# One planner setting: every engine's instruction order from the second machine model

## The chip, the cores and the metric

The program runs on one core of one Trainium2 chip. A core has five instruction streams that matter here: PE (TensorE, the matrix products; PEld is its weight loads), DVE (VectorE), ACT (ScalarE), POOL (GpSimd) and SP (SyncE, which here does nothing but issue DMA transfers). Each stream works off its own list in the order written into the program and waits at semaphores for the others. The metric is the device time in microseconds (us), from runs of one program.

## The reference, cut to what matters

One inference step of a two-layer trunk on 640 tokens (128 prompt, 512 latent) with 1024 features. For each layer: a normalised and modulated input `h`; one combined input projection `h @ w_in`; four token mixers side by side (a Mamba-2 scan, a retention, a grouped-query attention, a latent attention); each one's output times `w_br`, scaled by a sigmoid gate `h @ w_merge`, summed and multiplied by `w_out`; then a gated feed-forward with a width-3 convolution. The modulation is `silu(cond) @ w_mod + b_mod` with a `w_mod` of 1024 x 6144 per layer and two condition vectors.

```
h = rmsnorm(x, g_pre_mix) * (1 + sc_a) + sh_a
m = sum over 4 branches of sigmoid(h @ w_merge_b) * (branch_b(h) @ w_br_b)
x = x + g_a * rmsnorm(m @ w_out)
h = rmsnorm(x, g_pre_ffn) * (1 + sc_f) + sh_f
u = dwconv3(h @ w_ffn_up);  x = x + g_f * rmsnorm((silu(gate) * up) @ w_ffn_down)
```

## The kernel before

Activations lie feature-major: tiles of 128 features by 640 tokens. Every float32 operand of a linear layer is split exactly into a high and a low part, and a product is three matmuls of 320 columns (`lin_fm`, `lin_half`): high weights with both parts of the input, low weights with the high part. The weights come in 128 x 512 tiles: `weights` loads one from DRAM (`wr`, SP's queue, four buffers), ACT copies its high part (`wh`, line 305, four buffers), POOL subtracts for the low part (`wl`, line 308, three buffers). All matmuls are issued on line 321 (`mm`). Their results go to four PSUM banks (`lin`); three more (`st`) and one (`pv`) serve everything else.

The order of the program text is: the layer's input norm, the scan, the retention, the merge of branch 0, attention, merge 1, latent attention, merge 2, then `merge_out` (merge of branch 3, the output projection, two norms) and `ffn`. Two things are laid in between by hand:

- Steps that wait on a long chain (sums of a norm, chunks of the scans) are put on a list, `self.later`, and issued after a counted number of products of a linear layer (`go_on`; the constants `WAIT`, `RST`, `RHD`, `AWT`, `SWAIT`). The attention heads (`heads`, `head`, `maxima`) alternate the scores of one head with the row maxima of the next.
- The modulation products of later blocks are computed on DVE as a filler, two multiply-and-sum parts for each half row block (`mod_units`, line 584, output `wj`). Layer 1's modulation belongs to layer 0's last stages: `merge_out` and `ffn` call `fill(n)` at many places, and each half block's weights arrive in a tile `g` (five buffers) by a load on SP's queue, the queue that brings the `wr` tiles too.

What stands in the text is not yet the order on the chip. The library's planner takes the traced instructions and their dependencies, plays them on a model of the machine, and lists each engine's instructions (SP's loads among them) in the order in which the model started them. It does this twice: once taking ready instructions in the order of the text, and then, with each instruction's latest harmless start worked out from the first play, taking the ready one with the earliest of these. An instruction that is ready may so overtake others traced before it. Only two things hold it: data dependencies (a buffer's reuse is one of them), and order edges written by hand with `tc.issue_after`. All buffer counts are given in the kernel, so the planner does not choose them.

The edges are few. The helpers that write them are `go_on` and `behind` for PE and `fill`, which holds the filler's DVE work back only until the last input norm is done:

```
    def behind(self, on=True):
        return self.tc.issue_after(self.pe) if on else nullcontext()
```

```
        with self.tc.issue_after(self.last) if self.last is not None else nullcontext():
            for _ in range(n):
                if next(self.filler, 0) == 0:
                    break
```

Of the kernel before, what the change touches and what calls it, by code (L numbers as in the profile page):

```python
# [12 lines left out]
PSUM = bass.MemoryType.PSUM  # L13

D = 1024
T = 640
TP = 128
TL = 512
L = 2
# [7 lines left out]
# ---------------------------------------------------------------- host layout  # L27
FM_COLS = (
    [(512 + 128 * i, 128) for i in range(4)]        # 0-3   xs
    + [(1024, 128), (1152, 128)]                    # 4,5   B, C  # L30
    + [(128 * i, 128) for i in range(4)]            # 6-9   z
    + [(1296 + 128 * i, 128) for i in range(2)]     # 10,11 rq
    + [(1552 + 128 * i, 128) for i in range(2)]     # 12,13 rk
    + [(1808 + 128 * i, 128) for i in range(4)]     # 14-17 rv
    + [(2320 + 128 * i, 128) for i in range(4)]     # 18-21 rg
    + [(2832 + 128 * i, 128) for i in range(4)]     # 22-25 aq
    + [(3344, 128), (3472, 128)]                    # 26,27 ak, av
    + [(3600 + 128 * i, 128) for i in range(3)]     # 28-30 mcq
    + [(3984 + 128 * i, 128) for i in range(2)]     # 31,32 ckv
# [65 lines left out]
def _blk(w):  # L105
    """[L, K, M] -> [L, M/128, 128, K/128 * 128] (partition = k within its tile)."""
    l, k, m = w.shape
    return np.ascontiguousarray(
        w.reshape(l, k // 128, 128, m // 128, 128).transpose(0, 3, 2, 1, 4).reshape(l, m // 128, 128, k)
    )  # L110


def _cols(v):
    """[L, n*128] -> [L, 128, n]"""
    return v.reshape(v.shape[0], -1, 128).transpose(0, 2, 1)
# [98 lines left out]
# ---------------------------------------------------------------- the kernel  # L214
# [21 lines left out]
class Net:  # L236
# [14 lines left out]
    # ---- small helpers  # L251
# [83 lines left out]
    # ---- weights: float32 from DRAM, split exactly into two float32r parts  # L335
# [9 lines left out]
    def lin_fm(self, src, kt, xh, xl, m=128, unit=4, halves=((0, 320), (320, 640))):  # L345
        """w^T x by token halves: (PSUM [m, 320], their columns); src [128, kt * m] in DRAM, xh/xl lists of [128, tokens]"""
        p = [self.bank()[:m, : b - a] for a, b in halves]
# [14 lines left out]
    def lin_half(self, src, kt, xh, xl, m, done, hvs=(0,)):  # L362
        """done(w^T x [m, 320], half) for some token halves"""
# [17 lines left out]
    def lin_misc(self, src, kt, xh, xl, m, done, hvs=(0,)):  # L381
        """like lin_half for 48 outputs, the weights' two parts side by side: their products with xh in one pass,
        rows 0:48 and 64:112"""
# [22 lines left out]
    def lins(self, specs, full=0):  # L406
        """several linears whose first token half is wanted early: specs (src, kt, xh, xl, m, done);
        the first half of all of them comes first, the last one's weights serve both halves"""
# [9 lines left out]
    # ---- per-token factors from per-token sums, spread over the partitions  # L418
    def rsq(self, dst, src, scale, eps, mult=1.0):
        """dst = mult * (scale * src + eps)^-1/2 on small tiles"""  # L420
        m2 = 1.0 / (mult * mult)
        self.tsc(dst, src, scale * m2, eps * m2, ALU.mult, ALU.add)
        n = 1
# [7 lines left out]
    def rowsum(self, ss, scale, eps, mm=None, mult=1.0):  # L431
        """[128, 5]: mult * (scale * sum over the partitions + eps)^-1/2 per token"""
# [8 lines left out]
    def rowsum_later(self, ss, scale, eps, then):  # L441
        """then(R): the factors of the sums, spread, in steps between the products of other linears"""
# [16 lines left out]
    def spread(self, R, r, n):  # L459
        """R[p, 128 c + i] = r[i, c] on each partition p"""  # L460
# [8 lines left out]
    def selb(self, h):  # L469
        """[48, 128]: picks row h for the first 64 columns, row 8 + h for the others (rows 32.. the low parts)"""  # L470
        t = self.sbt(128, "selb", 2, F32R)
        self.act(t[:48].rearrange("p (a b) -> p a b", a=2), self.C("sel48", 48)[:, h : h + 9 : 8].unsqueeze(2).to_broadcast([48, 2, 64]))
        return t[:48]

    # ---- start
# [10 lines left out]
    def first(self):  # L486
        """x and the first norm: hh + hl = rmsnorm(x) * Am + S. S and Am come from TensorE, two feature tiles at a time,
        with silu(cond) [128, 2] as stationary"""
# [63 lines left out]
    # ---- modulation: silu(cond) @ w_mod, one output feature per partition  # L552
# [3 lines left out]
    def mod_units(self, l, blocks, halves, tile, pool=()):  # L556
        """the products of some output blocks, a part at a time"""
# [30 lines left out]
    def fill(self, n):  # L588
        """the next n parts of the filler, on DVE behind what it must not delay"""
# [8 lines left out]
    def mod_get(self, j, raw):  # L598
        """[128, 8, 2] of the six parts: product + bias"""
# [21 lines left out]
    # ---- norms  # L621
    def ss_add(self, ss, src, first, v=None):
        """ss += src^2"""
# [7 lines left out]
    def rs_half(self, sss, hv, scale, eps, then, mult=1.0, wait=5):  # L631
        """then(PSUM [128, 320]: mult * (scale * sum over the partitions of the sss + eps)^-1/2 of the half's tokens),
        in steps between the products of other linears"""
# [18 lines left out]
    def go_on(self, mm):  # L652
        """once per k tile of the linears, behind its products mm: a step that has waited long enough"""
# [13 lines left out]
    def flush(self, hvs=(0, 1)):  # L667
        """the steps left of some token halves"""
# [8 lines left out]
    def pre_half(self, x, sss, A, S, hh, hl, hv):  # L677
        """rmsnorm(x) * A + S of a token half, split"""
# [13 lines left out]
    def sq_add(self, sss, x, k, c):  # L692
        """the squares of x[k], added to the part of the engine that takes k"""
# [7 lines left out]
    def post_half(self, x, mo, ss, G, hv, then, squares=True, mult=1.0, old=None):  # L701
        """x = old (or x) + G * rmsnorm(mo / mult) of a token half; then(the new sums of squares)"""
# [14 lines left out]
    # ---- softplus on small tiles: max(x,0) + log1p(exp(-|x|))  # L717
# [17 lines left out]
    def conv_put(self, buf, p, hv):  # L735
        """half of a linear's output for the conv: prompt at 1..128, latent at 130..641, zeros around them"""
# [8 lines left out]
    def conv(self, buf, taps, bq):  # L745
        """centred width-3 conv over the tokens; the result has 641 columns: prompt at 0..127, latent at 129..640"""
# [12 lines left out]
    def silu_half(self, out, y, n, eng=None):  # L759
        """y holds half of the argument: out = (tanh(y) + 1) * y"""  # L760
# [4 lines left out]
    # ---- branch A  # L765
    def ssd(self, l, hh, hl):
# [5 lines left out]
        # dt  # L772
# [50 lines left out]
        # B, C  # L823
# [29 lines left out]
        # x  # L853
# [15 lines left out]
        # states  # L869
# [31 lines left out]
        # heads  # L901
# [46 lines left out]
    def gates(self, src, blocks, d):  # L948
        """2 * silu of a linear's outputs, kept in DRAM"""
# [31 lines left out]
    # ---- rope on [n, 512] latent columns  # L981
    def rotate(self, out, src, n, half, new=None):
        """out = src * cos + partner(src) * sin; src, out [n, 512]"""
# [8 lines left out]
    # ---- branch B  # L992
    def ret_in(self, l, hh, hl):
# [10 lines left out]
        # token-major, centred over the head's 128 values; those of the prompt also as they are  # L1004
# [17 lines left out]
    def ret_states(self, l, qk, vt):  # L1022
# [3 lines left out]
        # decays  # L1026
# [27 lines left out]
        # states  # L1054
# [52 lines left out]
    def ret(self, l, q, k, vt, Sin, Dr, QD, zd):  # L1107
        self.ph("ret.hd%d" % l)
        # heads by chunks; the outputs token-major, normalised as they are transposed
# [60 lines left out]
    # ---- attention over one head: queries q0:q0+nq, key tiles kts; scores^T = sum of lhsT/rhs pairs  # L1170
    def negmax(self, pairs, q0, nqt, k0, k1):
        """[128, nqt] = -max over keys k0..k1 of the scores, queries q0 + 128 i on partitions"""
# [15 lines left out]
    def maxrow(self, dst, nm, nqt, r0):  # L1188
        """dst [1, 128 nqt] (partition r0) = the columns of nm"""
# [6 lines left out]
    def probs(self, p, n, scale):  # L1196
        """exp(scale * p), split"""
# [8 lines left out]
    def maxima(self, kk, qq, q2, r0, wait):  # L1206
        """row r0 of q2 = -max of a head's scores per query, by steps"""
# [10 lines left out]
    def head(self, pairs, vh, vl, OP, SM, r_, scale, lag):  # L1218
        """a head's values and sums over the key tiles by steps; the latent's queries (columns 128:640) see the key columns
        128:768, the prompt's 0:128"""  # L1220
# [33 lines left out]
    def heads(self, n, maxima, head):  # L1254
        """the heads, each beside the maxima of the next one"""
# [7 lines left out]
    def attn_out(self, OP, SM, od, b, l, name):  # L1263
        """divide by the sums"""
# [5 lines left out]
    # ---- branch C  # L1270
    def att_in(self, l, hh, hl):
# [25 lines left out]
        # values  # L1297
# [13 lines left out]
    def att(self, l, raw, avT, r, od):  # L1311
# [27 lines left out]
        # normalised q, k  # L1339
# [54 lines left out]
    # ---- branch D  # L1394
    def mla_in(self, l, hh, hl):
# [3 lines left out]
        # low-rank q  # L1399
# [21 lines left out]
        # low-rank kv  # L1421
# [33 lines left out]
        # keys and values of all heads  # L1455
# [21 lines left out]
    def mla(self, l, qd, kd, vd, od):  # L1477
# [3 lines left out]
        # shared rotary key  # L1481
# [325 lines left out]
```

## Time and profile before

| what | us |
|---|---|
| three runs | 3084.05, 3086.69 (median), 3091.55 |
| the profiled execution, first to last instruction (span) | 3082.1 |
| PE busy in it | 2908.6 |
| DVE busy | 2002.3 |
| ACT busy | 1384.7 |
| POOL busy | 1141.6 |

The profiled execution is known by its span alone; the median of the runs is 4.6 us above it, which is what lies ahead of the first and behind the last instruction together with the difference from run to run. Busy time of PE is the union of its matmuls, which overlap each other; where it equals the length of a stretch, PE was never without a matmul in it. A wait is put down to the instruction that ended it.

### The profile page before, as it was taken

The page shows a single profiled execution, that of the slowest core. Times are in us where ns is not written, and L with a number is a line of the kernel's source. Part 1 is how long each engine was busy: PE and PEld are TensorE (multiplying, and loading weights), DVE is VectorE, ACT ScalarE, POOL GpSimd, SP SyncE. Part 2 cuts the span into 40 slices and gives each one's busy share as a digit, 9 for nine tenths or more (in the row PEclk, how much of TensorE's full clock was granted, in tenths as well). Part 3 has the DMA queues.
Part 4 walks back from the last instruction along what each step waited for, and adds up shares of the span by engine and source line. Part 5 has one row for each costly group of instructions (what it writes and reads, how often), then busy time and mean ns, then how long its engine had stood idle before and what let it go on. Part 6 is the DMA issues. An engine that isn't in the chain of part 4 may idle for free. (4 is left out here: it accounts for less than half of the span.)

```text
span 3082.1 us, 50945 instructions
## 1 busy us (share of the span) xinstructions
PE 2908.6 (94%) x18638; PEld 2721.2 (88%) x18638; DVE 2002.3 (65%) x3758; ACT 1384.7 (45%) x3013; POOL 1141.6 (37%) x889
## 2 busy tenths in 40 slices
PE   8999999999988988899988999999999999999998
PEld 4888898898888988899988899988988988999997
DVE  3678727637996599975576872177377455755556
ACT  3435246657634532233355353366476445433333
POOL 1223341131146643333364233411321566433334
PEclk9999999999999999999999999999999999999999
DMA  6215421143364435432243133211332433222223
GB/s 207 72 49 178 152 85 40 55 134 117 118 211 159 137 104 173 150 104 75 73 132 103 58 113 106 86 40 47 112 130 82 143 120 115 93 75 74 76 76 108
DMA packets 193418, 329.71 MB, mean 107 GB/s; under 512 B 20880, under 2 KB 54288, under 8 KB 193168
## 3 DMA queue, kind: packets, MB, share of 16 engines
q1 hardware_dynamic: 193168, 326.46, 32.5%
q8 instruction: 146, 2.39, 0.3%
q14 instruction: 104, 0.85, 0.1%
HBM read 293.41 MB, written 32.96 MB: 106 GB/s over the span
## 5 line engine op out<-in xcount | busy, mean ns | idle before, releaser
L308 POOL TENSOR_TENSOR wl<-wr,wh 128x512 fp32r<-128x512 f32 (+2 forms) x790 | 1068.9, 1357 | 1821.4 <-PE lin L321 1223.3
L321 PE MATMUL lin<-ah,wh 128*128 128x320 f32 (+1 forms) x3776 | 1176.2, 317 | 25.6 <-ACT wh L305 12.8
L321 PE MATMUL lin<-al,wh 128*128 128x320 f32 (+1 forms) x3776 | 1166.1, 315 | 13.3 <-DVE al L308 10.8
L321 PE MATMUL lin<-ah,wl 128*128 128x320 f32 x3744 | 952.0, 315 | 15.0 <-POOL wl L308 14.6
L305 ACT ACTIVATE wh<-wr 128x512 fp32r<-128x512 f32 (+2 forms) x796 | 487.5, 616 | 970.1 <-PE lin L321 522.9
L321 PEld LDWEIGHTS lin<-ah,wh 128*128 128x128 f32 (+1 forms) x3776 | 723.1, 192 | 43.1 <-ACT wh L305 16.8
L321 PEld LDWEIGHTS lin<-al,wh 128*128 128x128 f32 (+1 forms) x3776 | 721.3, 191 | 28.7 <-DVE al L308 14.2
L321 PEld LDWEIGHTS lin<-ah,wl 128*128 128x128 f32 x3744 | 657.5, 191 | 29.0 <-POOL wl L308 21.0
L308 DVE TENSOR_TENSOR m<-m,m 128x512 fp32r<-128x512 f32 (+6 forms) x393 | 317.3, 813 | 230.9 <-ACT m L305 225.3
L321 PE MATMUL lin<-K,wh 128*128 128x320 f32 (+1 forms) x1472 | 294.6, 313 | 9.4 <-ACT K L305 5.1
L305 ACT ACTIVATE m<-st 128x512 fp32r<-128x512 f32 (+2 forms) x480 | 223.3, 523 | 126.9 <-PE st L321 99.6
L321 PEld LDWEIGHTS lin<-K,wh 128*128 128x128 f32 x1472 | 238.4, 190 | 11.9 <-ACT K L305 5.6
L321 PE MATMUL lin<-O,wh 128*128 128x320 f32 x1024 | 214.7, 314 | 9.6 <-ACT O L305 4.6
L321 PE MATMUL lin<-K,wl 128*128 128x320 f32 (+1 forms) x736 | 185.5, 313 | 3.9 <-POOL wl L308 3.6
L321 PE MATMUL pv<-m,K 128*128 128x512 f32 (+2 forms) x832 | 184.1, 343 | 2.3 <-DVE m L308 2.1
L321 PEld LDWEIGHTS lin<-O,wh 128*128 128x128 f32 x1024 | 168.0, 190 | 15.8 <-DVE O L308 5.1
L584 DVE SCALAR_TENSOR_TENSOR wj<-g,silc 128x512 bf16<-128x512 f32 x160 | 146.9, 918 | 2.5
L321 PEld LDWEIGHTS pv<-m,K 128*64 128x64 f32 (+1 forms) x832 | 117.5, 160 | 26.5 <-DVE m L308 6.3
L584 DVE SCALAR_TENSOR_TENSOR wj<-K,silc 128x512 bf16<-128x512 f32 x160 | 138.9, 868 | 3.0 <-DMA K<-in_wmod 0.4
L321 PEld LDWEIGHTS lin<-K,wl 128*128 128x128 f32 x736 | 128.2, 189 | 5.6 <-POOL wl L308 5.4
L305 ACT ACTIVATE m<-m 128x641 f32<-128x641 f32 (+4 forms) x116 | 82.3, 713 | 112.7 <-DVE m L311 105.1
L321 PE MATMUL st<-Q,K 128*128 128x512 f32 (+3 forms) x480 | 131.7, 381 | 1.2 <-DVE nm L1182 0.8
(209 smaller groups left out, 3321.2 us busy)
## 6 DMA issues: line engine op xcount, KB each, us to landing
wr<-in_wup SPq DMA_DIRECT2D x196, 256.0 KB, 2.6
wr<-in_wmg SPq DMA_DIRECT2D x160, 256.0 KB, 2.6
wr<-in_win SPq DMA_DIRECT2D x142, 256.0 KB, 2.6
K<-in_wmod SPq DMA_DIRECT2D x112, 256.0 KB, 3.8
wr<-in_wdn SPq DMA_DIRECT2D x94, 256.0 KB, 2.7
wr<-in_wbr SPq DMA_DIRECT2D x80, 256.0 KB, 2.7
g<-in_wmod SPq DMA_DIRECT2D x80, 256.0 KB, 2.7
wr<-in_wout SPq DMA_DIRECT2D x64, 256.0 KB, 2.6
```

The source lines that it names most:

```text
L305: self.nc.scalar.activation(out, in_, func, **kw)
L308: (eng or self.nc.vector).tensor_tensor(out, a, b, op)
L321: self.pe = self.nc.tensor.matmul(out, lhsT, rhs, start=start, stop=stop).ins
L584: self.nc.vector.scalar_tensor_tensor(junk[:, :512], w[:, :512], 0.5, si, ALU.mult, ALU.mult, accum_out=acc)
```

## The change

The planner's model of the machine is exchanged: the same planner with the same two passes now plays the program on its second model, which follows each engine's queue of issued instructions and the semaphores between engines, instead of on the first. No instruction, buffer or edge is added or taken away. Which instruction follows which on PE, DVE, ACT, POOL and SP is drawn up anew, and so is which address a tile gets. The rest of the diff empties comments and docstrings, which are no instructions.

```
-    with _tile.TileContext(nc, auto_bufs=True) as tc:
+    with _tile.TileContext(nc, auto_bufs=True, schedule_with_timeline_sim=True) as tc:
         build(tc, A)
```

## Rows read from the trace of the kernel before

**Rows 1.** the page, part 1: busy us, share of the span, instructions.

```profile
span 3082.1 us, 50945 instructions
...
PE 2908.6 (94%) x18638; PEld 2721.2 (88%) x18638; DVE 2002.3 (65%) x3758; ACT 1384.7 (45%) x3013; POOL 1141.6 (37%) x889
```

**Rows 2.** the page, part 2: busy tenths, granted clock in 40 slices.

```profile
PE   8999999999988988899988999999999999999998
...
DVE  3678727637996599975576872177377455755556
...
PEclk9999999999999999999999999999999999999999
```

**Rows 3.** stretches of 77 us: length, PE, PEld, DVE, ACT, POOL, clock, DMA.

```profile
1155.00:1232.00 77.00, 66.96 (x425) 65.22 (x424) 75.54 (x161) 21.70 (x52) 27.46 (x17) 0.94 0.52 170
1232.00:1309.00 77.00, 67.49 (x429) 64.19 (x428) 76.31 (x165) 19.18 (x43) 29.12 (x19) 0.98 0.47 153
...
1386.00:1463.00 77.00, 77.00 (x527) 77.00 (x527) 42.70 (x68) 25.75 (x58) 28.66 (x22) 1.00 0.24 76
1463.00:1540.00 77.00, 77.00 (x527) 77.00 (x527) 43.46 (x68) 26.97 (x62) 27.93 (x22) 1.00 0.22 73
...
2695.00:2772.00 77.00, 77.00 (x527) 77.00 (x526) 41.82 (x66) 26.40 (x60) 28.43 (x22) 1.00 0.24 76
```

**Rows 4.** both feed-forwards, from first up-projection load to last down-projection load.

```profile
1052.70:1581.50 528.80, 492.45 (x3216) 481.31 (x3215) 411.41 (x782) 179.60 (x411) 222.81 (x162) 0.97 0.36 116
2577.00:3059.30 482.30, 474.82 (x3216) 472.11 (x3215) 278.88 (x442) 179.94 (x407) 208.25 (x163) 1.00 0.26 85
```

**Rows 5.** the same two stretches, instructions on the filler tile `wj` alone.

```profile
1052.70:1581.50 528.80, 148.24 (x320) 0.97 0.36 116
```

**Rows 6.** the filler by tile: duration ns min/median/max, first and last start.

```profile
L584 DVE SCALAR_TENSOR_TENSOR wj<-g,silc x160: 672/691/1818, 1098.2 to 1338.3; 128x512 bf16<-128x512 f32 x160
L584 DVE DVE_READ_ACCUMULATOR wj<-g,silc x160: 71/78/85, 1098.8 to 1338.9; 128x1 f32 x160
```

**Rows 7.** waits of SP's queue, 1140 to 1390 us: total, times, longest.

```profile
SPq L333 <- DVE wj L584: 122.9, 62, 6.0
SPq L333 <- POOL wl L308: 57.2, 19, 8.2
```

**Rows 8.** waits of SP's queue, 2700 to 3000 us.

```profile
SPq L333 <- POOL wl L308: 264.8, 85, 3.4
```

**Rows 9.** waits of all engines, 1140 to 1390 us.

```profile
POOL wl L308 <- ACT wh L305: 119.0, 36, 9.2
...
ACT wh L305 <- DMA wr<-in_wup: 34.1, 9, 6.3
```

**Rows 10.** groups on POOL, 1390 to 1540 us: busy, mean ns, idle before.

```profile
L308 POOL TENSOR_TENSOR wl<-wr,wh 128x512 fp32r<-128x512 f32 (+1 forms) x43 | 55.3, 1286 | 95.5 <-PE lin L321 90.8 <-ACT wh L305 4.7
```

**Rows 11.** attention heads, 470:630, 695:850, 2020:2180 and 2245:2400 together, all engines.

```profile
sum 630.00, PE 615.70 PEld 536.09 DVE 473.31 ACT 400.19 POOL 118.13; mean PE 153.93 PEld 134.02 DVE 118.33 ACT 100.05 POOL 29.53
```

**Rows 12.** the same four stretches, instructions on the tile `lin` alone.

```profile
470.00:630.00 160.00, 93.61 (x565) 85.93 (x565) 6.47 (x14) 7.71 (x16) 1.00 0.15 48
...
sum 630.00, PE 337.20 PEld 306.94 DVE 22.24 ACT 27.83; mean PE 84.30 PEld 76.73 DVE 5.56 ACT 6.96
```

**Rows 13.** waits of PE, whole span: total, times, longest.

```profile
PE st L321 <- DVE m L308: 31.7, 13, 5.6
PE lin L321 <- POOL wl L308: 20.1, 24, 1.4
PE lin L321 <- ACT wh L305: 13.9, 11, 5.3
...
PE st L321 <- DVE Q L308: 8.7, 8, 2.8
```

## The prediction, made before the changed kernel ran

> **What bounds the kernel now.** I read the page's busy times first, then its slices, then a table of stretches, and last the waits of the engines in the stretches that stand out. The busy times say PE: 2908.6 us of a span of 3082.1 us, DVE next with 2002.3 [rows 1]. So a mere reordering can win back at most the 173.5 us in which PE had no matmul, and a little more where it ran at the lower clock. The slices show where these are: PE is full in the second half of both feed-forwards and has most of its weak slices from the 12th to the 17th (847 to 1309 us), where DVE's digits are 9, 6, 5, 9, 9 and 9 [rows 2]. The table of stretches gives sizes: from 1386 to 1540 us PE is busy all 77.00 us of both stretches with 527 matmuls each (146 ns apiece), and no order can make that shorter; from 1155 to 1309 us it has 425 and 429, while DVE is busy 75.54 and 76.31 of 77 us [rows 3]. There DVE, or what DVE holds up, is the bound.
>
> Why there? The two feed-forwards are the same work, 3216 matmuls each by the table, but layer 0's takes 528.80 us and layer 1's 482.30 [rows 4]. What layer 0's has in addition is the filler: 160 parts of layer 1's modulation, 148.24 us of DVE with their accumulator reads [rows 5]. All of them start between 1098 and 1338 us, the first half of the feed-forward, though the text lays them out over nearly all of it [rows 6]. So the planner let them overtake, since they are ready early. The price is the 46.5 us between the two feed-forwards, and the chain of it is visible: SP's queue stands 122.9 us, 62 times, waiting for a part to release its `g` tile, with loads of `wr` queued behind [rows 7]; where there is no filler the same queue waits for weight buffers alone [rows 8]; ACT waits 34.1 us for the late `wr`, and POOL 119.0 us for ACT [rows 9]. The granted clock is part of the 46.5: 0.94 in the stretch from 1155 us, which mixes the 1.2 and the 2.4 GHz level, against 1.00 where PE was full before and during the stretch [rows 3].
>
> **The change, part by part.** It adds and removes no instruction. What moves is (a) the filler's parts and their loads, (b) the linear matmuls that are slipped between the steps of the attention heads, (c) the order inside the chains of the norms, (d) the rest of SP's, ACT's and POOL's lists, and addresses.
>
> (a) A model that follows queues and semaphores holds DVE longer for each instruction than one that does not, so it finds fewer idle moments on DVE early in layer 0's feed-forward, puts fewer parts there and sends their loads later on SP's queue. Is there room for them later? Layer 1's feed-forward leaves DVE 482.30 - 278.88 = 203.4 us idle [rows 4], more than the 148.24 us of all parts, so the whole 46.5 us could go. How many would move is not in the trace. I count what fits into the two full stretches behind the crowd: DVE is idle 34.30 + 33.54 = 67.8 us there [rows 3]; a part costs 148.24 / 160 = 0.927 us [rows 5]; 73 parts fit. If the loss goes with the number of parts that crowd, 73/160 of 46.5 = 21 us come back. The ends: 46.5 us gained, if all parts find cover; and below nothing, if they are packed still tighter, the rest of their 148.24 us uncovered, 148.2 - 46.5 = 102 us lost. I take the 21 us, the count from the nearest rows. The moved parts are not free of company: their cover is DVE's idle time beside a full PE. What would be late next is the convolution's work on DVE, which follows each pair of up-projections; it has the same 203 us of slack.
>
> The crowded and the full stretch differ little in POOL's load: 27.46 against 28.66 us of 77 [rows 3]. A part takes 691 ns in the median and up to 1818 [rows 6]; in the full stretch POOL's splits are each preceded by idle time, 95.5 us for 43 of them, 90.8 of it waiting for PE to free a buffer [rows 10]. That is 2.2 us ahead of each split, so a part that stood in its way for 0.69 us would be hidden. The Trainium skill (SBUF — State Buffer, "Who interferes with whom") says that a VectorE instruction with two SBUF inputs and a GpSimd instruction that reads SBUF exclude each other, and whichever issues second is blocked for the whole of the other. By that rule, and without the cover, the 73 moved parts would hold 73 x 0.69 = 50 us of splits in a stretch where PE has no gap to give, and the sum of this edit would be a loss of 29 us; the idle time in [rows 10] speaks against it.
>
> (b) In the four stretches of heads PE is busy 615.70 of 630.00 us [rows 11], and 337.20 us of that are linear matmuls that the text places after the heads [rows 12]: the planner draws them in when a head's step is not ready. The best end is the 14.3 us of idle time; the worst is the second rival's. I take nothing, since 97.7% busy is nearest to the first end and there is little to improve.
>
> (c) PE's longest waits by name are for DVE before the sums of the norms (31.7 us in 13 waits), for POOL's and ACT's splits (20.1 and 13.9), and before a head's first score (8.7) [rows 13]. The first and last are serial chains: sums, power, spread, multiply. No order shortens them; nothing. The waits for the splits lie mostly in the crowd of (a) and are counted there.
>
> (d) In the full stretches the order can change at will at no cost as long as the weights stay ahead; the cover is POOL's 2.2 us per split. If it went, every split that is late would cost PE what it is late by, up to 1.3 us. Addresses cost nothing that this trace could show.
>
> The sum is made against the profiled execution: 3082.1 - 21 = 3061, and with the 4.6 us by which the median of the runs lies above that span, 3066 us.
>
> **The rivals.** First, nothing to speak of moves: many of PE's steps hang on hand-written edges and on data, and the second model may price a part on DVE as the first does. For it: PE is 94% busy [rows 1]; against it: all 160 parts had been free to move and did move [rows 6]. Time 3087. Here also belongs the case that the setting acts on the first play alone and the lists come out nearly alike.
>
> Second, on the other side: the heads run out of linear matmuls. If the second model sees a head's chain through ACT and DVE as longer, it draws in the matmuls of the following merge faster, and the last heads of each eight have none left. Price: heads without the work on `lin` keep DVE busy 473.31 - 22.24 = 451 us, 0.716 of the 630, and PE at least 615.70 - 337.20 = 278.5, or 0.442 [rows 11, 12]. If the last quarter of the heads is bare, it takes at least 0.716 x 157.5 = 113 us; the rest of PE's work, 615.7 - 0.442 x 157.5 = 546 us, comes before it; 659 in place of 630 is 29 us more: 3116. If the last half is bare, 225.5 + 476.5 = 702, and the time is 3159. It decides from the point where the bare share x loses more than the present idle time, 630 x (0.716 - 0.442) x = 14.3, x = 8%: less than one head of eight. Against it: the first order spreads them evenly, with about 0.58 of PE's time in the first stretch [rows 12], on no better knowledge.
>
> Third, also slower: a model with queues lets an engine take up ready work while the one before still runs, and parts are what is ready. If they crowd into DVE's queue still earlier, ahead of convolution work that comes ready a moment later, a further quarter of their 148.24 us is uncovered, 37 us: 3124. It decides as soon as the 240 us from the first to the last part shrink.
>
> Fourth, more than forecast: all 46.5 us and some of the heads' 14.3 come back, 3040 or less.
>
> **How the numbers follow.** Forecast, 3066 with its own range 3045 to 3077: 0.40. First rival 0.17, second 0.22, third 0.13, fourth 0.08. Differences within 0.3%, 9 us, are what a measurement of this kernel cannot tell from no change. So faster 0.48, same 0.17, slower 0.35. The range 3030 to 3140 leaves out the far part of the fourth rival (0.03) and of the second and third (together 0.13).
>
> **What would show it.** Right: the parts' last start in layer 0's feed-forward moves from 1338 us towards its end; SP's wait for them falls well below 122.9 us; the feed-forward of layer 0 comes down from 528.8 to about 508 us while layer 1's stays near 482. The heads' four stretches together stay within 15 us of 630. Wrong: a feed-forward of layer 0 as long or longer; or stretches at the end of the heads where PE falls to about 0.6 busy and no matmul on `lin` is seen; or new gaps in the full stretches, where PE had none, because a split of weights or its load comes late on an engine's new list.

## The result, and the profile after

The changed kernel takes 3252.59 us in the median of four runs (3250.28 to 3255.31) against 3087.93 for the kernel before (3084.05 to 3091.55): 1.053 times as long, 95% interval 1.0518 to 1.0547. The forecast was 3066 us with a range up to 3140, so it was wrong in sign and the range did not hold the time. The loss lies in the mixer stages of both layers. Most of it has the mechanism of the second rival, whose size was forecast too small; the rest arose in the scans, which no rival had named.

From the page of the changed kernel: span, busy times, PE's slices and the granted clock in 40 slices of 81 us.

```profile
span 3252.9 us, 50914 instructions
...
PE 2981.3 (92%) x18638; PEld 2769.5 (85%) x18638; DVE 1987.0 (61%) x3758; ACT 1387.2 (43%) x3013; POOL 1136.8 (35%) x889
...
PE   8997999899978989999979979998989799899997
...
PEclk9998999899988999999989989999999899999999
```

Against [rows 1] the instructions of each engine are the same and the span is 170.8 us longer. PE is busy 72.7 us more with the same 18638 matmuls, at a mean granted clock of 0.946 against 0.977, and idle 98.1 us more. Sevens and eights stand in the 4th and 8th slice and in the 24th, 28th, 30th, 32nd and 35th, where [rows 2] had nines; all but the last lie in the mixers.

The two feed-forwards, first up-projection load to last down-projection load; then a full stretch of layer 0's; then the filler's tiles in it; then SP's wait for them (total, times, longest).

```profile
1119.60:1648.20 528.60, 493.03 (x3215) 485.44 (x3213) 410.43 (x779) 180.84 (x414) 224.37 (x162) 0.96 0.38 116
2740.40:3225.70 485.30, 475.03 (x3209) 472.82 (x3208) 272.73 (x435) 179.85 (x407) 207.86 (x163) 0.99 0.27 83
```

```profile
1453.00:1530.00 77.00, 77.00 (x527) 77.00 (x527) 42.33 (x68) 25.75 (x58) 28.62 (x22) 1.00 0.25 76
```

```profile
L584 DVE SCALAR_TENSOR_TENSOR wj<-g,silc x160: 675/684/1836, 1165.1 to 1419.4; 128x512 bf16<-128x512 f32 x160
```

```profile
SPq L333 <- DVE wj L584: 126.9, 57, 5.9
```

Against [rows 4, 6, 7] almost nothing has moved: the stage takes 528.60 us where it took 528.80, the parts start over 254 us in place of 240, SP waits 126.9 us in place of 122.9. So all that was argued about the feed-forwards concerns work that the change left where it was. The mixers, from the start to the first load of the output projection and from the end of layer 0's feed-forward to the same point of layer 1, are 64.9 and 102.6 us longer: 167.5 of the 170.8.

The built programs show why. The table counts, for the attention heads of layer 0 (360 matmuls on PE) and the latent heads (400), how many other matmuls stand in PE's list beside each eighth of them. The first eighth of the attention also holds what comes ahead of the heads.

| matmuls of others per eighth of the heads | |
|---|---|
| attention, list of before | 124, 50, 53, 49, 51, 52, 56, 26 |
| attention, list of after | 299, 167, 134, 0, 0, 0, 0, 28 |
| latent, list of before | 54, 37, 43, 84, 67, 45, 50, 21 |
| latent, list of after | 120, 156, 143, 163, 6, 0, 6, 0 |

In the first list the merges' linear products are dealt out over the heads, some fifty to each. In the second they crowd into the first heads until there is none left: the 4th to 7th of eight attention heads stand bare (with no product of a linear layer beside them), and the last four latent heads but for a dozen products, in both layers. Why the second model plays it so is not in any trace and stays open; the experiments below are about what the list costs. The scan's heads lose theirs too: beside the last two of eight stand 41 and 6 in layer 0, and 0 and 6 in layer 1, where before they had 39 to 50.

A stretch of the changed kernel's bare attention heads: all engines, then the tile `lin` alone, then what was waited for in it.

```profile
588.00:657.00 69.00, 52.65 (x221) 35.85 (x220) 48.46 (x89) 40.65 (x88) 0.00 (x0) 0.88 0.06 21
```

```profile
588.00:657.00 69.00, 0.00 (x0) 0.00 (x0) 0.00 (x0) 0.00 (x0) 0.88 0.06 21
```

```profile
ACT m L305 <- PE st L321: 16.5, 13, 2.8
DVE K L311 <- PE st L321: 8.7, 2, 4.4
PEld st L321 <- DVE Q L308: 7.7, 2, 4.1
PE st L321 <- DVE Q L308: 6.8, 2, 3.7
```

No engine is full: PE 52.65 of 69 us, DVE 48.46, ACT 40.65, POOL without an instruction. Each waits for another; the head's chain goes round through PE, ACT and DVE. The granted clock is 0.88, a mixture of the 2.4 and the 1.2 GHz level, where the covered heads before had 1.00. In the trace the middle attention heads of the kernel before took 16.3 to 18.6 us each with their fifty products; these bare ones take 14.8 to 16.9. Taking out fifty products, 7.3 us of PE, made a head shorter by one to two us. Where they went they cost their full time: the second and third attention head of layer 0 hold some 300 products in the changed kernel's trace and take 63.1 us, where they held some 100 and took 35.0, which is 0.14 us for each one more.

### The profile page after: what moved, and what is told of

Its sections match the earlier page's. It is cut to its first block, busy times and chain, and to the rows that moved or that the text cites. A ratio compares the mean times of both kernels' runs of the same rounds, so it can differ in the third digit from the quotient of the medians.

```text
span 3252.9 us, 50914 instructions
## 1 busy us (share of the span) xinstructions
PE 2981.3 (92%) x18638; PEld 2769.5 (85%) x18638; DVE 1987.0 (61%) x3758; ACT 1387.2 (43%) x3013; POOL 1136.8 (35%) x889
## 4 chain that ended last, share of the span: by engine, by line
PE 68%; DVE 21%; issue 5%; DMA 3%; ACT 3%; POOL 1%; SPq 0%; POOLq 0%; DVEq 0%; ACTq 0%
PE lin L321 55%; PE st L321 8%; DVE m L311 5%; DVE wj L584 4%; PE pv L321 4%; DVE m L308 3%; DVE X L308 2%; ACT m L305 2%; DVE m L318 1%; DVE K L308 1%; DVE al L311 1%; DVE nm L1182 1%; DMA g<-od 1%; DMA K<-in_wmod 1%; DVE O L308 0%
## 5 line engine op out<-in xcount | busy, mean ns | idle before, releaser
L321 PEld LDWEIGHTS lin<-al,wh 128*128 128x128 f32 (+1 forms) x3776 | 718.5, 190 | 37.6 <-DVE al L308 14.8
L308 DVE TENSOR_TENSOR m<-m,m 128x512 fp32r<-128x512 f32 (+6 forms) x393 | 307.9, 792 | 205.4 <-ACT m L305 199.1
L321 PE MATMUL lin<-K,wh 128*128 128x320 f32 (+1 forms) x1472 | 305.5, 316 | 16.3 <-ACT K L305 9.4
L321 PE MATMUL pv<-m,K 128*128 128x512 f32 (+2 forms) x832 | 201.0, 370 | 24.5 <-DVE m L308 21.3
L321 PE MATMUL lin<-K,wl 128*128 128x320 f32 (+1 forms) x736 | 196.4, 316 | 4.2 <-POOL wl L308 4.2
L321 PEld LDWEIGHTS pv<-m,K 128*64 128x64 f32 (+1 forms) x832 | 130.7, 175 | 59.1 <-DVE m L308 30.3
L1182 DVE TENSOR_REDUCE nm<-st 128x1 f32<-128x320 f32 (+1 forms) x288 | 125.2, 463 | 79.6 <-PE st L321 77.6
L321 PE MATMUL st<-Q,K 128*128 128x512 f32 (+3 forms) x480 | 148.2, 421 | 7.3 <-ACT Q L305 4.7
```

The lines of the kernel that those rows point to most:

```text
L308: (eng or self.nc.vector).tensor_tensor(out, a, b, op)
L321: self.pe = self.nc.tensor.matmul(out, lhsT, rhs, start=start, stop=stop).ins
L1182: self.nc.vector.tensor_reduce(t[:, j * 8 + i : j * 8 + i + 1], p[:, :w], AX.X, ALU.max, negate=True)
```

## The experiments

**Whose list is it?** All instructions keep their names between the two builds, so a list can be carried over: order edges without a semaphore tie each instruction of an engine behind the one ahead of it in the other kernel's list (the code is shortened). The edges stand when the planner plays, so it draws the lists of the other engines anew around the tied one.

```
+def in_order(tc):
+    for text in ORDERS:                      # one list per engine
+        for n in numbers(text):
+            if last is not None:
+                tc.add_manual_dep(ins[n], last.name, no_sync)
+            last = ins[n]
     build(tc, A)
+    in_order(tc)
```

First, second model with PE's list of before. 

> Second model for everything, but PE's list is tied by order edges, instruction behind instruction, to the list that the first model made; DVE, ACT, POOL, SP and the addresses stay the second model's. Theory A (the loss is PE's list alone: the linear products are drawn ahead of the steps of the heads, and the last heads are left bare): the heads get their products back, 3088 us give or take 15, and the stages from merge 0 to the output projection come back to about 541 and 519 us. Theory B (the lists of DVE, ACT, POOL and SP slow the heads' chains, and PE's gaps only follow): 3200 us or more. In between, the shares are read off.

Measured: 3100.14 us, 1.004 times before (1.0025 to 1.0055). With PE's list 152.5 of the 164.5 us come back; what the second model makes of the rest costs 12. That rest is not the changed kernel's own. In the traces ACT's list holds at 78% of its places the same kind of instruction (operation, tiles and shape) as in the kernel before, and at 50% the same as in the changed kernel; those two agree at 47%. For DVE it is 57%, 41% and 38%. So it is PE's list that decides, in part through the lists that are drawn around it.

The opposite. 

> The opposite: first model for everything, PE's list tied to that of the second. Theory A: 3253 us give or take 20, with the last five of eight attention heads bare. Theory B: below 3130 us, since the other engines keep the lists that were fast.

Measured: 3287.11 us (ratio 1.063 to 1.0662), so theory A again, and 34.5 us beyond the changed kernel itself. The other lists are again drawn around PE's (ACT's agrees with the changed kernel at 85% of its places, with the kernel before at 50%); those of the first model fit PE's second list worse than the second model's do. Theory A had not expected that much. Its rival, that the other engines would keep the lists that were fast, was not put to the test as it was meant, since they did not keep them.

Then by part. 

> Second model, PE's list of the first only within the attention, the latent attention and merges 1 and 2 of both layers. Theory A: from the end of merge 0 to the first product of the output projection the traces have 540.9 + 518.5 = 1059.4 us before and 591.5 + 575.6 = 1167.1 after, so 107.7 us come back: 3145 us. Theory B: 3253 us, nothing comes back. If the scans are to blame for most of it: above 3200.

> Second model, PE's list of the first only within the scan, the retention and merge 0 of both layers. Theory A: up to the end of merge 0 the traces have 396.1 us before and 411.3 after in layer 0, and 350.8 against 389.8 from layer 1's first product, so 54 us come back: 3198 us. Theory B: 3253 us. If this run's and the last run's gains add up to e1's, the parts are independent; if not, a list made in one part decides over the other.

Measured: 3141.03 and 3207.97 us, 111.6 and 44.6 us less than the changed kernel. Together 156.2, where the whole list gave 152.5: the two parts add up. The expectations were 107.7 and 54.

The four stretches from the first row maximum to the last value product of the heads: in the kernel before, in the changed one, and with the list carried over for the heads.

```profile
sum 561.20, PE 551.53 PEld 472.17 DVE 440.62 ACT 369.73 POOL 90.52; mean PE 137.88 PEld 118.04 DVE 110.16 ACT 92.43 POOL 22.63
```

```profile
sum 774.50, PE 706.06 PEld 598.17 DVE 467.38 ACT 407.78 POOL 129.90; mean PE 176.51 PEld 149.54 DVE 116.84 ACT 101.94 POOL 32.47
```

```profile
sum 584.60, PE 553.07 PEld 469.05 DVE 440.30 ACT 367.75 POOL 87.91; mean PE 138.27 PEld 117.26 DVE 110.07 ACT 91.94 POOL 21.98
```

The heads of the changed kernel are 213 us longer, but hold more products than before; what counts is the stage with what lies around it, 107.7 us.

What the scans lose is seen in PE's waits for DVE, in the row that leads [rows 13]: changed kernel, then heads carried over, then scans carried over.

```profile
PE st L321 <- DVE m L308: 63.9, 23, 6.6
```

```profile
PE st L321 <- DVE m L308: 66.8, 24, 6.6
```

```profile
PE st L321 <- DVE m L308: 34.0, 15, 6.9
```

Before it was 31.7 us [rows 13]. The time comes back with the scans' list and not with the heads'. It is 32 of the 44.6 us.

**Can the products be spread by hand?** Each k tile of the merges, and of the retention's inputs, gets an edge behind a step of the heads.

```
+    def pace(self, free, tiles):
+        n = len(self.ends)                   # last matmul of every step of the heads
+        self.holds = [None] * free + [self.ends[i * n // tiles] for i in range(tiles)]
 in lin_fm, for each k:
+                hold = self.holds.pop(0) if self.holds else None
+                with self.tc.issue_after(hold) if hold is not None else nullcontext():
                     ... the k tile's products
```

> Second model, no list copied: the k tiles of merges 1 and 2 get order edges that spread them behind the steps of the attention heads (16 and 8 tiles free, the others evenly), and those of the retention's products behind the steps of the scan's heads (32 free, 64 spread). The edges only hold back; all else is left to the second model. Theory A (what matters is where the products stand beside the heads, not the rest of PE's list): at least half of the 165 us come back, below 3170 us, and no head is bare but the last. Rival (the gain of the copied list lies in its fine order): above 3210 us.

Measured: 3165.55 us, 1.0249 times before (1.0231 to 1.0266). 87 us come back, just over half, which theory A asked for and no more. Evenly dealt is better than greedily taken, but the first order, which puts a product where a step is not ready, is better by another 76 us, 64 after the 12 that the rest costs. Which of its differences from the even spread is worth that, no run separates.

**Does DVE's list carry the last 12 us?** PE's and DVE's lists of before, the rest the second model's. 

> As the first experiment, second model with PE's list of the first, and DVE's list of the first too; ACT, POOL, SP and addresses stay the second's. The first experiment left 12 us. If DVE's list carries them: 3088 us give or take 5. If they lie in ACT's, POOL's or SP's lists or in the addresses: 3100.

Measured: 3104.33 us (ratio 1.0034 to 1.0064). No: with DVE's list exactly that of before nothing is gained. The 12 us lie in ACT's, POOL's or SP's lists or in the addresses, which was not taken further.

**What does a bare head cost?** Merges 1 and 2 are left out and what follows the heads is held behind them, so all 32 heads are bare; then products that nobody reads go behind every step.

```
             while next(a, 0) | next(b, 0):
-                pass
+                o = self.bank()
+                for k in range(2):                       # none, 2 or 4
+                    with self.behind():
+                        self.mm(o[:, :320], self.hx[k][:, :128], self.hx[k][:, :320])
```

> First model; merges 1 and 2 are left out in both layers, and the products that follow the heads are held behind them, so that all 32 attention and latent heads are bare. It gives the pace of a bare head. By DVE's busy time, as in the prediction's second rival: 0.716 of a covered one, some 12 to 13 us where the trace of before has 16.3 to 18.6 in the middle of the attention heads. By the last five heads of the changed kernel: 15 to 17 us, at a granted clock of 0.8 to 0.9.

> The same with 24 products of 320 columns in each head that nobody reads, two behind each step; PE does one in 0.146 us where it is full, so 3.5 us more of PE a head. If the half clock is what makes the bare heads slow: the granted clock rises towards 1.00 and the heads get shorter, up to 1.6 to 3.3 us each, 50 us or more on the whole. If the chain through ACT and DVE sets the pace: the heads stay as long as without them, or get longer by up to 3.5 us each, 0 to 112 us on the whole.

> The same with 48 products in each head, four behind each step: about what the first order gives a head. If products beside a head are free up to what fits into its chain's waits, the heads take 15 to 18 us, no more than 2 us above the bare ones, though PE has 7.0 us more to do in each; if each product costs its time, 32 x 7.0 = 224 us more than the run without them.

The first of the four stretches and their sum, with no, 24 and 48 products in a head.

```profile
464.80:588.40 123.60, 95.39 (x397) 66.91 (x397) 85.87 (x162) 72.47 (x156) 0.00 (x0) 0.84 0.04 13
...
sum 511.30, PE 394.94 PEld 279.70 DVE 376.90 ACT 313.91 POOL 3.73; mean PE 98.74 PEld 69.92 DVE 94.22 ACT 78.48 POOL 0.93
```

```profile
467.60:594.60 127.00, 110.95 (x586) 89.73 (x586) 86.49 (x162) 73.52 (x157) 0.00 (x0) 0.93 0.04 13
...
sum 531.50, PE 464.89 PEld 374.27 DVE 383.82 ACT 317.86 POOL 3.74; mean PE 116.22 PEld 93.57 DVE 95.95 ACT 79.46 POOL 0.93
```

```profile
464.10:610.90 146.80, 136.90 (x777) 117.32 (x777) 87.92 (x162) 74.67 (x157) 0.00 (x0) 0.94 0.03 11
...
sum 607.30, PE 565.35 PEld 484.58 DVE 395.96 ACT 323.49 POOL 3.69; mean PE 141.34 PEld 121.15 DVE 98.99 ACT 80.87 POOL 0.92
```

So 511.3, 531.5 and 607.3 us. By the same view of `lin` alone they hold 5, 765 and 1525 products. So the first 760 (111 us of PE at 0.146 us each) cost 20 us, and the next 760 cost 76. The clock rose from 0.84 to 0.93 with the first ones and the heads did not get shorter, so nothing in these runs gives the half clock as the pace of a bare head. They fit a chain through PE, ACT and DVE that sets it, with room beside it for about half of what the first order puts there, if the products are pinned behind every step. Pinned so, 48 cost 96 us; the first order, which pins none, has as many in the heads for half of that. A gain from the clock that the added products eat up again is not excluded. The whole kernels took 2946.83, 2968.81 and 3037.39 us.

The kernel before has 1552 products in its four stretches and needs 561.2 us: 49.9 us above the bare ones, 0.032 us for each product, where a product costs 0.146 us with nothing else to do [rows 3]. By these two means, taking one away from beside a head and doing it elsewhere loses 0.114 us, an estimate. By the lists 206 products left the last five eighths of the attention in each layer, and 171 and 156 the last four of the latent heads: 739 x 0.114 = 84 us, of the 107.7 (by the traces) to 111.6 us (by the run) that the heads lost. The other quarter is not accounted for one by one; in the latent heads of layer 0 the filler's parts stand beside bare heads.

**Was step (a) right about the filler?** The change did not move the parts, so they were moved by hand, in the kernel before.

```
                 self.act(fh[f][:, d], sg[:, s])
-                self.tt(fl[f][:, d], sg[:, s], fh[f][:, d], ALU.subtract)
+                self.last = self.nc.vector.tensor_tensor(fl[f][:, d], sg[:, s], fh[f][:, d], ALU.subtract).ins
 and the same at the accumulations of the down-projection: fill() holds its parts behind self.last
```

> First model; each of the filler's parts in layer 0's feed-forward is held on DVE behind the DVE work that the text has ahead of it, so that the parts spread into its second half. Step (a) of the prediction (the crowd costs the 46.5 us, and what finds cover later comes back): 21 to 46 us less, 3042 to 3067 us, layer 0's feed-forward at 482 to 508. Rival (the parts cost what they cost wherever they stand, or the 46.5 us are not theirs): 3088 us or more.

Measured: 3098.4 us, 1.0032 times before (1.0022 to 1.0042): 9 us slower. The parts start over 367 us in place of 240, and the rival holds. Then layer 1's products left out (the filler is emptied, its results set to zero).

> First model; layer 1's modulation products (all 192 half blocks' parts that run in layer 0's merge 3 and feed-forward) are left out and their results set to zero. If the filler is the price of layer 0's feed-forward: that stage comes down from 528.8 to about 482 us and the whole to 3042 or a little less. If the 46.5 us have another cause (the stage's start, the loads): the stage stays above 510.

Measured: 3024.57 us; the stage comes to 482.0 us, and another 10.9 us are gone ahead of it, where the first parts run. So the 46.5 us are the filler's, as the prediction said, and yet they don't come back where the parts are spread. Two more runs on the spread version split a part into its load and its DVE time.

```
+                    if l == 0 or j == 0:            # layer 1: one load per half for all 48 blocks
+                        w = self.modw(F32) if l == 0 else self.sbt(512, "wk", 1)
+                        self.load(w[:, :512], ...)
 or, with all loads,
-  scalar_tensor_tensor(junk[:, :512], w[:, :512], 0.5, si, ...)
+  scalar_tensor_tensor(junk[:, :8], w[:, :8], 0.5, si[:, :8], ...)
```

> First model, layer 1's parts held as in e6_fill_held, but each half reads one resident tile of weights in place of its 48 loads (the loads are left out, so layer 1's modulation is another one): the parts keep their DVE time and their places, SP's queue never waits for one. Theory S (SP's queue is the price: loads of weights stand behind loads that wait for a part to free its tile): layer 0's feed-forward comes from 536.5 to 482 to 495 us, the whole to about 3050. Theory D (the parts' time on DVE, between the convolutions and the accumulations that the splits and the banks wait for, is the price): the stage stays above 520.

> The opposite, also on e6_fill_held: all loads stay and each part frees its tile at the same place of DVE's list, but multiplies 8 columns in place of 512 (the other columns are left out), so it costs DVE a tenth. Theory D: 482 to 495 us for layer 0's feed-forward. Theory S: above 515, since SP's queue waits at the same places; some of it must go in any case, as DVE comes to the parts sooner.

Measured: 3095.25 and 3045.53 us. Layer 0's feed-forward of the four, in this order: held, no filler, held without loads, held with short parts.

```profile
1058.00:1594.50 536.50, 500.04 (x3216) 482.22 (x3215) 428.46 (x782) 179.60 (x411) 220.41 (x162) 0.97 0.37 114
```

```profile
1041.80:1523.80 482.00, 474.40 (x3217) 471.72 (x3216) 281.05 (x454) 180.59 (x409) 207.65 (x163) 1.00 0.28 85
```

```profile
1052.90:1590.80 537.90, 499.45 (x3216) 480.79 (x3215) 428.60 (x782) 179.75 (x411) 221.03 (x163) 0.97 0.24 77
```

```profile
1050.90:1538.90 488.00, 477.68 (x3216) 474.41 (x3215) 337.14 (x782) 182.12 (x411) 213.27 (x163) 0.99 0.39 125
```

With one load per half left SP waits for a part once, 11.2 us in the stage, where it was 131.0 in 56 waits, and the stage is as long; with all loads and a third of the parts' DVE time (48.7 us in place of 147.5) it is 488.0 us. DVE's time is the price, theory D, although DVE is busy only 428 of 538 us. What waits for it is seen between 1213 and 1521 us: no filler, then held without loads.

```profile
ACT K L305 <- DVE m L308: 24.5, 14, 1.9
POOL wl L308 <- ACT wh L305: 12.2, 6, 2.8
...
ACT Q L305 <- DVE Q L318: 0.2, 1, 0.2
```

```profile
POOL wl L308 <- ACT wh L305: 109.9, 37, 9.3
...
ACT Q L305 <- DVE Q L318: 71.7, 37, 12.5
ACT K L305 <- DVE m L308: 51.2, 13, 4.2
```

`DVE Q` is an instruction of one or two columns that writes the zeros at the ends of a convolution's tile; it takes some 150 ns, and ACT's copies of the product into the same tile come behind it:

```profile
L318 DVE TENSOR_SCALAR Q<-lin x52: 142/152/156, 1217.9 to 1520.8; 128x2 f32<-128x2 f32 x26, 128x1 f32<-128x1 f32 x26
```

With parts ahead of it ACT stands 71.7 us where it stood 0.2, up to 12.5 us at a time; behind ACT wait the weights' high parts and behind these POOL's low parts. That this wait is the main link is read from the waits; no run removed it alone.

The parts also made other work of DVE longer. One of the convolution's multiply-adds, as a group on DVE in layer 0's feed-forward: the kernel before, the parts held, and a third of the parts on POOL (the next experiment).

```profile
L311 DVE SCALAR_TENSOR_TENSOR m<-Q,pc,m 128x641 f32<-128x641 f32 x38 | 37.1, 976 | 0.8
```

```profile
L311 DVE SCALAR_TENSOR_TENSOR m<-Q,pc,m 128x641 f32<-128x641 f32 x38 | 50.4, 1327 | 1.3
```

```profile
L311 DVE SCALAR_TENSOR_TENSOR m<-Q,pc,m 128x641 f32<-128x641 f32 x38 | 55.5, 1460 | 1.3
```

The traces show why, instruction by instruction. The stage has 76 such multiply-adds. With the parts held, 33 of them start while a split runs on POOL. Each of these ends 0.68 to 0.69 us after the split's end and takes 1.78 to 1.95 us; the 40 with nothing on POOL beside them take 0.89. Of the 160 parts 46 start so and take 1.47 us in the mean, the 84 with nothing beside them 0.69. So DVE stands some 70 us behind POOL, an estimate from these means; in the kernel before, with 6 multiply-adds and 42 parts, it is 43 us.

**A version that beats both?** If DVE's time is the price, POOL and ACT might do parts: an existing argument of `mod_units` sends every third one there, or two of three.

```
-self.filler = self.mod_units(1, range(48), ((0,), (1,)), self.sil_tile)
+self.filler = self.mod_units(1, range(48), ((0,), (1,)), self.sil_tile, (0,))      # or (0, 1)
```

> First model; every third part of layer 1's modulation is multiplied on POOL and summed on ACT instead of DVE. If DVE's time is the price of the filler (148 us of it cost 46.8 us of the stage in the run without filler, 0.316 us each): 49 us less of it give 15 us, 3072 us. Rival (POOL's splits of the weights are late behind the parts, each of which takes POOL about as long as a split, 1.29 us in the trace): 3088 us or more.

> As the last, with two of three parts on POOL and ACT. DVE's time the price: 31 us less than before, 3057 us. Rival: slower than before, and slower than with one third.

Measured: 3095.89 us (1.0013 to 1.0032) and 3145.05 us (1.0158 to 1.0202). The rival holds both times, and its mechanism is seen in PE's waits for POOL's low parts around this stage: before, with a third of the parts on POOL, with two thirds.

```profile
PE lin L321 <- POOL wl L308: 13.0, 15, 1.4
```

```profile
PE lin L321 <- POOL wl L308: 26.3, 16, 4.2
```

```profile
PE lin L321 <- POOL wl L308: 48.5, 15, 10.6
```

With a third of the parts on POOL layer 0's feed-forward takes 529.4 us, as long as before, and starts 16.2 us later, where the parts begin, in a profiled execution that is 12.7 us longer; with two thirds it takes 577.6. The 49 us less of DVE did not come about: with 53 parts fewer DVE is as busy as before, 412.69 us against 411.41 [rows 4], since 46 of the 76 multiply-adds now start while POOL runs and the parts left on DVE take 1.07 us in the mean. So this run is no test of what DVE's time costs. A part takes DVE 691 ns in the median with nothing in its way [rows 6] and POOL 1718 in the mean. The stage with every third part on POOL, and groups on POOL from 1000 to 1650 us:

```profile
1068.90:1598.30 529.40, 490.72 (x3216) 483.19 (x3215) 412.69 (x676) 213.71 (x517) 311.47 (x215) 0.96 0.38 115
```

```profile
L308 POOL TENSOR_TENSOR wl<-wr,wh 128x512 fp32r<-128x512 f32 (+1 forms) x204 | 281.3, 1384 | 239.8 <-PE lin L321 119.9 <-ACT wh L305 110.6 <-issue 4.1
L308 POOL TENSOR_TENSOR m<-g,silc 128x512 f32<-128x512 f32 x53 | 90.2, 1718 | 10.8 <-DMA g<-in_wmod 6.7 <-DVE silc L311 4.1
```

No run that computes the whole result was faster than the kernel before.

## Why the prediction was wrong, step by step

**Step (b) failed, "I take nothing, since 97.7% busy is nearest to the first end and there is little to improve".** That is where most of the loss arose: the heads lost 107.7 to 111.6 us, where nothing was put down. The stretch was judged by what an order could gain there. But a stretch that is full only because 337 us of movable work lie in it [rows 11, 12] has everything to lose from a new order. The argument against the second rival, that the first order spreads the products evenly "on no better knowledge", was no argument about the second model at all: the even spread was a property of the first one's play.

**The second rival had place, sign and sign-post right and its price too low.** Its sign-post, stretches at the end of the heads with PE at about 0.6 and no product on `lin`, is the stretch from 588 to 657 us (0.76 busy). Its price was 29 to 72 us for a quarter to a half; the heads lost 107.7 to 111.6 with half of them bare. The mis-sized term is DVE's 0.716: a bare head was taken to run as fast as DVE's busy time allows. In the runs the bare heads need 511.3 us where the covered ones need 561.2, 0.91, with DVE busy 376.90 of the 511.3, 0.74: they are slower than any engine's busy time asks for, as a serial chain would be. With 0.91 in its place the rival's own sum for the last half gives 0.91 x 315 + 476.5 = 763 us, 133 more than 630, now somewhat above what was lost. And the scans, 44.6 us more, stood in no sum: step (b) and the rival looked at the heads of [rows 11] alone.

**Step (a) failed twice.** The planner did not move the parts: a longer DVE time per instruction was expected of the second model, and the 240 us became 254. And the premise, 21 us back from spreading, is refuted: spread by hand they cost 9 us more. What failed is the cover, DVE's idle time beside a full PE, with POOL's 2.2 us per split: what comes late by the waits is first of all a two-column instruction on DVE that an eviction waits for, and DVE itself is held up, since its multiply-adds wait for splits that run. The 0.927 us that the sum takes for a part holds such waiting already: 0.918 us in the mean without the accumulator's read, against 0.69 where nothing is in the way. SP's 122.9 us [rows 7], read as the chain of the loss, are a symptom: with the parts held, the stage is as long without them.

The prediction weighed the rule of the Trainium skill (SBUF — State Buffer, "Who interferes with whom") for the splits alone, 50 us less the gain. The traces agree with the rule, and in both directions: multiply-adds on DVE end a fixed time behind the split that ran, as shown above, and in the held run the 68 splits that start while DVE runs an instruction with two inputs in SBUF take 1.54 us in the mean, the 21 with none beside them 1.30. That is 16 us of POOL in the stage, where POOL is busy 220.41 us, against the 70 us of DVE. The prediction counted the smaller of the two.

**Step (c), nothing for the norms' chains,** overlooked that a chain which no order shortens can lose what runs beside it. It also took the whole row of 31.7 us for sums of the norms. By the traces 9 of its 13 waits are that, 23.4 us; the other four are products of the scans and the retentions. In the changed kernel the row has 63.9 us, 35.3 of them ahead of sums and 28.6 ahead of such products, which had no order of their own in the prediction.

**Step (d) held.** The full stretch above is as full as before, 527 matmuls in 77.00 us.

The first rival was wrong about the mixers and right about the feed-forwards. The third, ready work taken up too early, named the right habit for the wrong engine: it was PE's products that came early, not DVE's parts.

## What to carry to other kernels

A stretch that is full because an order mixes a long serial chain with free work has to be priced by what it would cost to lose the mixture, not by its idle time: count the free pieces and take their time alone minus their time beside the chain (here 0.146 and 0.032 us). A scheduler that takes whatever is ready spends that free work early; before trusting a new order, count how many pieces stand beside each step of the chain in its list. And idle time of an engine is no cover for added work if others wait for short instructions of it, or if its instructions and another engine's hold each other up: what decides is who stands behind those instructions, and whether they get longer when the two engines run side by side.

## What the runs showed that was not expected

- 24 products in each bare head, 111 us of PE in all, cost 20 us; the next 24 cost 76. The granted clock went from 0.84 to 0.93 with the first, and the heads did not get shorter.
- One list is not good or bad by itself: PE's second list with what the first model draws around it took 3287.11 us, longer than either model's own set.
- DVE at 428 us of 538 busy was what a feed-forward with PE at 500 us waited for; SP's wait for the parts was not.
- A multiply-add on DVE that starts while a split runs on POOL ends 0.68 to 0.69 us after the split does, 1.78 to 1.95 us in place of 0.89. Moving parts from DVE to POOL therefore left DVE as busy as it was.
